# Attention stage of a streaming encoder step: query tiles in the keys' pool, 12 gate blocks ahead, one head's division on ScalarE, LayerNorm sums on GpSimd, the merge kept in PSUM banks

## The chip, the cores and the metric

The kernel runs on one core of one Trainium2 chip. The metric is device time in microseconds of one launch. Three runs of the kernel before took 2397.39, 2404.95 and 2409.07 us; the median is 2404.95 us. Engines are named as the profile names them: PE (TensorE, with PEld for its weight loads), DVE (VectorE), ACT (ScalarE), POOL (GpSimd), and SP, whose queue issues every DMA of this kernel.

## The reference: what is computed

One layer of a streaming encoder on 1024 prompt frames and 64 sample frames (which see 128 cached frames), model width 1024:

```python
h = x + 0.5 * swiglu(rms(x, ffn1_norm), ffn1_w_in, ffn1_w_out)
u = rms(h, mix_norm)
q, k, v, qi, ki, wi, conv_in, gate = split(u @ w_in)
# branch A: per query keep the top 256 keys (48 for the sample) by the indexer's score
attn = softmax(q k^T / 8 over the kept keys) v            # 8 heads of 64, 2 key heads
# branch B
c  = ca * sigmoid(cb)                                     # conv_in = [ca | cb], 512 channels
dc = causal_depthwise_conv31(c) + conv_b
conv_out = silu(layernorm(dc, ln_g, ln_b)) @ conv_w_out
g_a, g_c = split(sigmoid(gate + b_gate))                  # 1024 columns each
h = h + (g_a * (attn @ attn_w_out) + g_c * conv_out) @ w_out
h = h + 0.5 * swiglu(rms(h, ffn2_norm), ffn2_w_in, ffn2_w_out)
y = rms(h, final_norm)
```

It also returns the new keys, values, indexer keys and the last 30 convolution rows.

## The kernel before, in words

Activations lie transposed: channels on the 128 partitions, frames along the free dimension. Every product is done in three passes with operands split in a high and a low part (`mm3`, L135 to L138: high by high, high by low, low by high); ACT makes the high part (L118, L152), DVE or POOL the low part (L119, L153). Outside the attention stage the frames are cut in four blocks of 272; in and around it in three chunks of 364, 362 and 362 (`CHUNKS`).

The program has five stages: the first FFN; the input projection with the indexer scores and the convolution; the search for each query's threshold (DVE, with branches on the data that handle ties, L972 to L1029); the attention stage; and the rest (the last merge and output projection, the second FFN, the final norm). The change lies in the attention stage and just ahead of it.

**Gates.** A gate block (`gates`, L1046) is one 128-column block of the gate weights: per chunk, 8 x 3 = 24 matmuls into a PSUM bank, a tanh by ACT from that bank (L1052, tile `sg`), and a DMA of it to DRAM (L1053). There are 16 blocks of three such steps. `GPRE` = 14 of them run ahead of the attention stage, beside the search on DVE; the other two run inside it.

**Attention.** A unit (`Pair`) is one query tile and two heads; tiles are taken in the order 7, 6, 8, 5, 4, 3, 2, 1, 0, four units each. `soft` (L1079) makes a unit's probabilities: scores by PE into one of three `lg` banks (L1099, L1100), mask added and maximum taken by DVE into tile `pr` (L1102, a custom operation), maximum scaled by DVE (L1110), exponential with its sum by ACT for each of the two heads (L1112), reciprocals by DVE (L1114), and the division: head 0 by POOL, head 1 by DVE (L1116, `SC = 'PV'`). `turn` (L1119) transposes one slot (up to two blocks of 128 keys of both heads) on PE into one of two `pt` banks (L1126) and splits it: high part by ACT (tile `ph`), low part by DVE (tile `pl`). `values` (L1138) multiplies by the values two slots later (L1146, L1147) and sends the result to DRAM. There are 84 slots. The queries of a tile are loaded by `load_q` (L683): four DMAs into `raw`, a cast by ACT (L691) and a subtraction by DVE (L692) into tile `qt`. The first tile's `qt` comes from pool `ak`, which also holds the keys; the next one's from `ap_`, the attention pool, which is opened after the search's pools are closed; then they alternate. Each pool has one.

**Fill.** After each slot `fill` (L1328) advances other work, so that PE has something to do while a unit's softmax is under way. `RATE` says how many steps per slot: 0.75 in `conv_part` (the LayerNorm of chunk 2 beside the last two gate blocks, seven steps; then `conv_out` of the three chunks, eight steps of 12 matmuls each, beside the LayerNorms of the other two), 0.7 in `merge_part` (`merge` of chunk 2, nine steps of which eight have 12 matmuls, and `wout` of chunk 2, eight steps of 24), 2.0 in `last_part` (`merge` of chunk 1). A merge waits until its chunk's query tiles are done (`need_of`, `ready`). The fill's results go through two PSUM banks (`psf`).

**LayerNorm** (`norm`, L1182). The chunk comes from DRAM as four channel tiles (`lx`); DVE adds two pairs (L1189); PE sums over the partitions with a matrix of ones (L166, `colsum`); PE spreads the mean back (L175); DVE adds it (L1198), ACT squares (L1199), DVE adds pairs again (L1200), PE sums, DVE takes the reciprocal root and scales by it and the gain (L1211); then ACT takes tanh (L1213), and two DVE operations with the bias make x + b times (1 + tanh) (L1214, L1216); then the split (L152, L153, tiles `ch`, `cl`).

**Merge** (`merge`, L1244). Per 128 columns: gate `ga` and the stored convolution part `mpt` come from DRAM, PE projects the attention result into a bank `p` (`ps` in the profile), DVE makes (1 + ga) * p into `ga` (L1263) and adds half of `mpt` (L1264), then the split (tiles `xh`, `xl`).

The order of instructions on each engine is fixed when the program is built, by a scheduler that works from its own estimate of durations; each engine runs its list in order and waits on semaphores. A wait that the scheduler did not foresee therefore holds everything that stands behind it on that engine.

## Time and profile before

| | us |
|---|---|
| median of three runs | 2404.95 (2397.39 to 2409.07) |
| the profiled execution, its own time | 2402.76 |
| its span, first to last instruction | 2400.7 |
| PE busy in the span | 2296.5 (96%) |
| DVE busy | 1696.4 (71%) |
| POOL busy | 1412.6 (59%) |
| ACT busy | 1169.0 (49%) |
| mean granted PE clock | 0.984 |

The first score matmul of the attention stage starts at 1233.21 us of the span, and the last value matmul at 1543.21 us. In the rows below, `out<-in` are tiles by the program's names, `x24` a count, and "idle before" the time that the engine stood still just ahead of such instructions, with the one whose end released them. PE's busy time is that of overlapping matmuls; a run of equal matmuls is better priced from start to start. In a table of windows the columns are the busy time of PE, its weight loads, DVE, ACT and POOL, then the granted PE clock (1.00 is full), the share of the DMA engines and GB/s.

### The profile page before, as it was taken

What the parts mean: (1) busy time and instruction counts of PE and PEld (TensorE: products, weight loads), DVE (VectorE), ACT (ScalarE), POOL (GpSimd) and SP (SyncE); (2) the same over time, 40 slices, a digit from 0 to 9 for tenths busy, and PEclk for the clock granted to TensorE, in tenths of its full rate; (3) what the DMA queues carried; (4) which work ended last, traced back from release to release, by engine and by line L of the source; (5) the groups of instructions that cost most, each with busy time, mean ns of one, the idle gap of its engine ahead of it and who ended that gap; (6) DMA issues with size and microseconds to landing.
All of it is one profiled execution on the core that took longest, in us unless ns stands there. A gap on an engine that the chain in (4) does not pass through costs nothing.

```text
span 2400.7 us, 44002 instructions
## 1 busy us (share of the span) xinstructions
PE 2296.5 (96%) x16610; PEld 2266.0 (94%) x16610; DVE 1696.4 (71%) x3776; ACT 1169.0 (49%) x2238; POOL 1412.6 (59%) x873
## 2 busy tenths in 40 slices
PE   7999999999999999999799989799999999999998
PEld 6999999999999999999788888799999999999997
DVE  7766667766668387689727977768666678676666
ACT  6333445444436446887345555545433444434343
POOL 5455555555557786879754455457555555545554
PEclk9999999999999999999999989999999999999999
DMA  5332233223223444233233456653222321332233
GB/s 192 106 108 94 95 100 125 89 89 106 90 92 127 138 127 135 83 120 120 67 99 98 144 164 178 212 172 111 83 94 99 105 101 62 124 107 93 94 97 117
DMA packets 130407, 273.44 MB, mean 114 GB/s; under 512 B 17936, under 2 KB 77200, under 8 KB 130192
## 3 DMA queue, kind: packets, MB, share of 16 engines
q1 hardware_dynamic: 130192, 270.61, 35.0%
q8 instruction: 131, 2.15, 0.4%
q14 instruction: 84, 0.69, 0.1%
HBM read 231.87 MB, written 38.75 MB: 113 GB/s over the span
## 4 chain that ended last, share of the span: by engine, by line
PE 42%; DVE 5%; DMA 2%; issue 1%; ACT 0%; POOL 0%; DVEq 0%; SPq 0%; ACTq 0%
PE ps L136 13%; PE ps L138 13%; PE ps L137 13%; PE pt L1126 1%; DMA ga<-d_g 1%; PE ps L166 1%; DVE pr L1102 1%; PE pv L1146 0%; DVE pl L153 0%; PE pv L1147 0%; DVE ga L1264 0%; PE lg L1099 0%; DMA ar<-d_at 0%; PE lg L1100 0%; DVE t L211 0%
## 5 line engine op out<-in xcount | busy, mean ns | idle before, releaser
L119 POOL TENSOR_TENSOR wlo<-raw,whi 128x1024 fp32r<-128x1024 f32 (+1 forms) x187 | 438.5, 2350 | 360.6 <-ACT whi L118 353.0
L136 PE MATMUL ps<-x,wp 128*128 128x272 f32 x1760 | 506.4, 289 | 3.0 <-ACT wp L152 2.9
L137 PE MATMUL ps<-x,wp 128*128 128x272 f32 x1760 | 505.1, 288 | 0.0
L136 PE MATMUL ps<-x,whi 128*128 128x272 f32 (+2 forms) x1544 | 483.3, 313 | 22.7 <-ACT sg L1052 14.0
L138 PE MATMUL ps<-x,wp 128*128 128x272 f32 x1760 | 503.4, 290 | 1.4 <-DVE wp L153 1.1
L138 PE MATMUL ps<-x,wlo 128*128 128x272 f32 (+2 forms) x1544 | 481.5, 312 | 0.0
L137 PE MATMUL ps<-x,whi 128*128 128x272 f32 (+2 forms) x1334 | 412.9, 310 | 0.9 <-POOL x L153 0.9
L136 PE MATMUL ps<-gh,whi 128*128 128x272 f32 x1408 | 400.0, 289 | 6.8 <-DVE spare L284 5.0
L137 PE MATMUL ps<-gl,whi 128*128 128x272 f32 x1408 | 405.2, 289 | 0.0
L138 PE MATMUL ps<-gh,wlo 128*128 128x272 f32 x1408 | 404.2, 289 | 0.0
L153 POOL TENSOR_TENSOR wlo<-raw,whi 128x1024 fp32r<-128x1024 f32 x88 | 219.5, 2495 | 258.8 <-ACT whi L152 258.8
L136 PEld LDWEIGHTS ps<-x,wp 128*128 128x128 f32 x1760 | 331.2, 188 | 3.9 <-ACT wp L152 3.8
L138 PEld LDWEIGHTS ps<-x,wp 128*128 128x128 f32 x1760 | 328.8, 188 | 2.9 <-DVE wp L153 2.3
L137 PEld LDWEIGHTS ps<-x,wp 128*128 128x128 f32 x1760 | 331.4, 188 | 0.0
L136 PEld LDWEIGHTS ps<-x,whi 128*128 128x128 f32 x1544 | 293.6, 190 | 25.4 <-ACT sg L1052 14.7
L153 POOL TENSOR_TENSOR wp<-s,wp 128x512 fp32r<-128x512 f32 x176 | 257.2, 1462 | 98.3 <-ACT wp L152 98.2
L118 ACT ACTIVATE whi<-raw 128x1024 fp32r<-128x1024 f32 (+1 forms) x187 | 190.6, 1020 | 226.2 <-PE ps L137 103.4
L680 POOL TENSOR_TENSOR ac<-ac,pd 128x559 f32<-128x559 f32 x180 | 264.6, 1470 | 53.5 <-ACT pd L679 27.6
L428 DVE SCALAR_TENSOR_TENSOR h<-ps,h 128x272 f32<-128x272 f32 x384 | 164.3, 437 | 186.3 <-PE ps L138 185.6
L138 PEld LDWEIGHTS ps<-x,wlo 128*128 128x128 f32 x1544 | 293.5, 190 | 1.0
L136 PEld LDWEIGHTS ps<-gh,whi 128*128 128x128 f32 x1408 | 263.6, 189 | 7.9 <-DVE spare L284 5.5
L138 PEld LDWEIGHTS ps<-gh,wlo 128*128 128x128 f32 x1408 | 266.3, 189 | 0.0
(254 smaller groups left out, 4818.9 us busy)
## 6 DMA issues: line engine op xcount, KB each, us to landing
raw<-wf SPq DMA_DIRECT2D x337, 512.0 KB, 3.4
raw<-wf SPq DMA_DIRECT2D x32, 384.0 KB, 3.2
d_g<-sg SPq DMA_DIRECT2D x32, 181.0 KB, 1.9
d_h<-h SPq DMA_DIRECT2D x2, 2176.0 KB, 10.8
y<-t SPq DMA_DIRECT2D x32, 136.0 KB, 1.9
raw<-d_q SPq DMA_DIRECT2D x32, 128.0 KB, 3.1
raw<-d_qi SPq DMA_DIRECT2D x24, 128.0 KB, 3.0
d_g<-sg SPq DMA_DIRECT2D x16, 182.0 KB, 3.6
```

What stands on the lines that cost most here:

```text
L118: nc.scalar.activation(hi[:, :n], raw[:, :n], AF.Copy)
L119: self.weng.tensor_tensor(lo[:, :n], raw[:, :n], hi[:, :n], op=ALU.subtract)
L136: t.matmul(out, wh, xh, start=first, stop=False)
L137: t.matmul(out, wh, xl, start=False, stop=False)
L138: t.matmul(out, wl, xh, start=False, stop=last)
L153: (eng or nc.vector).tensor_tensor(lo, x, hi, op=ALU.subtract)
L166: self.nc.tensor.matmul(ps[:, b * P:(b + 1) * P], x[:, t0:t0 + P], self.ones, start=i == 0, stop=i == len(tiles) - 1)
L428: nc.vector.scalar_tensor_tensor(x, p, 0.5, x, op0=ALU.mult, op1=ALU.add)
L680: nc.gpsimd.tensor_tensor(ac, ac, pd, op=ALU.add)
L1102: nc.vector.tensor_tensor_reduce(p[:, b * pw:(b + 1) * pw], o, bias[:rows, bo:bo + pw], 1.0, -3e38, op0=ALU.add, op1=ALU.max, accum_out=mb ...
L1126: nc.tensor.transpose(pt[:kn, o:o + r], u.pr[hh][:, kk:kk + kn], ident[:r, :r])
```

## The change

Seven edits, all in or around the attention stage:

1. `load_q` of the attention takes its `qt` from `ak`, two buffers there, for all tiles; none is in `ap_`.
2. `GPRE` 14 becomes 12: four gate blocks instead of two run inside the attention stage.
3. The fill has five parts instead of three. `gate_part` runs five gate steps alone, then the LayerNorm of chunk 2 beside the other seven; `conv_part` is the convolution's projection; `merge_part` and `wout_part` are apart; `RATE` is 0.5, 1.0, 1.0, 0.5, 1.0 steps per slot.
4. Head 1's division goes from DVE to ACT (a copy with a scale per row).
5. The two pair sums of each LayerNorm go from DVE to POOL.
6. The LayerNorm's bias: ACT adds it (`Identity` with a bias), and one DVE operation multiplies by (1 + tanh), in place of two DVE operations.
7. In `merge`, the first DVE operation writes its result back into the PSUM bank, and the second reads it there.

```diff
-SC = 'PV'
-GPRE = 14
+GPRE = 12
-RATE = (0.75, 0.7, 2.0)
+RATE = (0.5, 1.0, 1.0, 0.5, 1.0)
...
-                    qts[u.i] = load_q(ak, d_q, u.t0, rows, (ak, ap_)[AORD.index(u.i) % 2], 1)
+                    qts[u.i] = load_q(ak, d_q, u.t0, rows)
...
-                            for e in range(2):
-                                {'P': nc.gpsimd, 'V': nc.vector}[SC[e]].tensor_scalar(u.pr[e], u.pr[e], sm[:rows, e:e + 1], None, op0=ALU.mult)
+                            nc.gpsimd.tensor_scalar(u.pr[0], u.pr[0], sm[:rows, 0:1], None, op0=ALU.mult)
+                            nc.scalar.activation(u.pr[1], u.pr[1], AF.Copy, scale=sm[:rows, 1:2])
...
-                nc.vector.tensor_tensor(s[:, 0:2, :], x[:, 0:2, :], x[:, 2:4, :], op=ALU.add)
+                nc.gpsimd.tensor_tensor(s[:, 0:2, :], x[:, 0:2, :], x[:, 2:4, :], op=ALU.add)
...
-                nc.vector.tensor_tensor(s[:, 0:2, :], s[:, 0:2, :], s[:, 2:4, :], op=ALU.add)
+                nc.gpsimd.tensor_tensor(s[:, 0:2, :], s[:, 0:2, :], s[:, 2:4, :], op=ALU.add)
...
-                    nc.vector.scalar_tensor_tensor(s[:, t, :], x[:, t, :], par("lnb", t), s[:, t, :],
+                    nc.scalar.activation(x[:, t, :], x[:, t, :], AF.Identity, bias=par("lnb", t))
+                    nc.vector.scalar_tensor_tensor(x[:, t, :], s[:, t, :], 1.0, x[:, t, :],
                                                    op0=ALU.add, op1=ALU.mult)
-                    nc.vector.scalar_tensor_tensor(x[:, t, :], x[:, t, :], par("lnb", t), s[:, t, :],
-                                                   op0=ALU.add, op1=ALU.add)
...
-                    nc.vector.scalar_tensor_tensor(ga, ga, 1.0, p, op0=ALU.add, op1=ALU.mult)
-                    nc.vector.scalar_tensor_tensor(ga, mpt, 0.5, ga, op0=ALU.mult, op1=ALU.add)
+                    nc.vector.scalar_tensor_tensor(p, ga, 1.0, p, op0=ALU.add, op1=ALU.mult)
+                    nc.vector.scalar_tensor_tensor(ga, mpt, 0.5, p, op0=ALU.mult, op1=ALU.add)
...
+            def gate_part():
+                steps = gates(gorder[GPRE:], ak, 2)
+                for _ in range(3 * (16 - GPRE) - 7):
+                    next(steps)
+                    yield
+                lp = C["pool"] = self.pool(cx, "ln", 1)
+                yield from both(norm(2, lp, lp), steps)
+                act_es.close()
...
-            parts = [conv_part(), merge_part(), last_part()]
-            need_of = (None, 2, 1)
+            parts = [gate_part(), conv_part(), merge_part(), wout_part(), last_part()]
+            need_of = (None, None, 2, None, 1)
```

How the built programs differ at the places that matter, engine by engine. A row is an instruction with its line, the tiles it writes and reads, and the semaphores on which it waits; `DVE_sequencer` is one that DVE raises when it has left the search's branches. Lines between L35 and the LayerNorm's sums are one lower in the changed kernel.

First, ACT at the end of the search, before. The row with L691 is the cast of the second query tile; L972 is the place of the search's branch on ACT; L679 belongs to the convolution, L118 to the gates' weights.

```order
L118 ACTIVATE whi<-raw 128x1024 [waits DMAHW4_49,PE_49]
L1052 ACTIVATE sg<-ps,hb 128x362 [waits DMAHW2_49,PE_49]
L679 ACTIVATE pd<-ci,par 128x559 [waits Pool_49] x2
L972 UNCONDITIONAL_BRANCH
L1052 ACTIVATE sg<-ps,hb 128x364 [waits DMAHW3_49,PE_49]
L691 ACTIVATE qt<-raw_15467 128x1024 [waits DVE_sequencer_49,DVE_49]
L679 ACTIVATE pd<-ci,par 128x559 [waits Pool_49] x2
L1052 ACTIVATE sg<-ps,hb 128x362 [waits DMAHW5_49,PE_49]
```

And ACT in the changed kernel, where that cast (now L690) stands, among the search's last rounds (L892 to L895).

```order
L892 ACTIVATE bias,cnt<-Y,cand 128x1024 [waits Activation_49]
L678 ACTIVATE pd<-ci,par 128x559 [waits Pool_49]
L894 ACTIVATE flag<-cnt,thx 128x1 [waits Activation_49]
L678 ACTIVATE pd<-ci,par 128x559 [waits Pool_49]
L690 ACTIVATE qt<-raw_15176 128x1024 [waits DMAHW6_49,DMAHW7_49,DMAHW2_49,DMAHW1_49]
L895 ACTIVATE hibx<-flag,cand 128x1 [waits Activation_49]
L117 ACTIVATE whi<-raw 128x1024 [waits DMAHW5_49,PE_49]
L1051 ACTIVATE sg<-ps,hb 128x362 [waits DMAHW4_49,PE_49]
```

The cast has moved from behind the branch to 52 rows ahead of it, and waits only for its DMAs; its subtraction on DVE moves into the search with it. Behind the branch, which stands on ACT's row 1023 now and on 1021 before, there are only convolution and gate rows.

Second, PE a little after the first scores, before: scores, the LayerNorm's sum (L166), scores, gates.

```order
L1099 MATMUL lg<-kh_13693,qt 128x512 [waits DVE_49]
L1100 MATMUL lg<-kl_13694,qt 128x512
L138 MATMUL ps<-x,wlo 128x364
L1099 MATMUL lg<-kh_13693,qt 128x512 [waits DVE_49]
L1100 MATMUL lg<-kl_13694,qt 128x512
L166 MATMUL ps<-ones,ls 128x128 [waits DMAHW3_49,DMAHW4_49,DMAHW2_49,DMAHW5_49,DMAHW1_49,DMAHW6_49,DMAHW0_49,DMAHW7_49,DVE_sequencer_49,DVE_49]
L166 MATMUL ps<-ones,ls 128x128 x7
L1099 MATMUL lg<-kh_13693,qt 128x512 [waits DVE_49]
L1100 MATMUL lg<-kl_13694,qt 128x512
L136 MATMUL ps<-x,whi 128x362 [waits Activation_49]
```

And PE in the changed kernel at its first transposes (L1125).

```order
L137 MATMUL ps<-x,wlo 128x362
L135 MATMUL ps<-x,whi 128x364 [waits Activation_49]
L136 MATMUL ps<-x,whi 128x364
L137 MATMUL ps<-x,wlo 128x364 [waits Pool_49]
L135 MATMUL ps<-x,whi 128x364
L1125 MATMUL pt<-ident,pr 128x128 [waits DVE_sequencer_49,Pool_49]
L1125 MATMUL pt<-ident,pr 128x128 x7
L1098 MATMUL lg<-kh_13702,qt 128x512 [waits DVE_49]
```

The first score matmul stands on PE's row 8401 before and on 8257 now: 144 gate matmuls (six steps of 24) that stood ahead of it stand behind it. In the changed kernel 19 gate matmuls stand between the third and the fourth score tile, 76 between the first score and the first transpose, and the first LayerNorm sum comes 110 rows after that transpose.

Third, POOL ahead of its first division (L1116, now L1114), before.

```order
L119 TENSOR_TENSOR wlo<-raw,whi 128x1024 [waits DMAHW0_49,PE_49,Activation_49]
L680 TENSOR_TENSOR ac<-ac,pd 128x559 [waits Activation_49,Pool_49] x6
L119 TENSOR_TENSOR wlo<-raw,whi 128x1024 [waits DMAHW4_49,PE_49,Activation_49]
L119 TENSOR_TENSOR wlo<-raw,whi 128x1024 [waits DMAHW7_49,PE_49,Activation_49] x2
L1116 ISA
L1116 TENSOR_SCALAR pr<-pr,sm 128x1024 [waits DMAHW3_49,DVE_sequencer_49,DVE_49]
```

And POOL there in the changed kernel; L1188 is the first LayerNorm sum.

```order
L118 TENSOR_TENSOR wlo<-raw,whi 128x1024 [waits DMAHW3_49,PE_49,Activation_49]
L679 TENSOR_TENSOR ac<-ac,pd 128x559 [waits Activation_49,Pool_49] x6
L118 TENSOR_TENSOR wlo<-raw,whi 128x1024 [waits DMAHW0_49,PE_49,Activation_49]
L1188 TENSOR_TENSOR ls<-lx 128x784 [waits DMAHW2_49,DMAHW3_49,DMAHW1_49,DMAHW4_49,DMAHW0_49,DMAHW5_49,DVE_sequencer_49,DMAHW6_49,DVE_49,DMAHW7_49,Activation_49,Pool_49]
L1114 ISA
L1114 TENSOR_SCALAR pr<-pr,sm 128x1024 [waits DVE_49] x2
```

The LayerNorm sum, which waits for its load from DRAM, now stands in POOL's list ahead of the first division; the later five sums stand between divisions (L1114) and the weights' low parts (L118) in the same way.

More of the change, by code (lines that the diff above doesn't have):

```diff
@@ L1041, in run @@
             AORD = TORD
-            qts = {AORD[0]: load_q(ak, d_q, *ATILES[AORD[0]][:2], qb=1)}
+            qts = {AORD[0]: load_q(ak, d_q, *ATILES[AORD[0]][:2])}
             gorder = [(m, self.woff()) for m in (*range(8, 16), *range(8))]
@@ L1297, in both @@
                     yield
-            def conv_part():
-                with ExitStack() as es:
-                    lp_ = self.pool(es, "ln", 1)
-                    yield from both(norm(2, lp_, lp_), gates(gorder[GPRE:], ak, 2))
-                    act_es.close()
-                    lq = self.pool(es, "lnq", 1, side="right")
+            cx = ExitStack()
+            def gate_part():
[6 more added lines that the diff above has]
+                act_es.close()
+            def conv_part():
+                lp_ = C["pool"]
+                with cx:
+                    lq = self.pool(cx, "lnq", 1, side="right")
                     for c, q in ((2, lq), (1, lp_), (0, None)):
@@ L1311, in merge_part, with wout_part @@
                 yield from merge(2, self.mp)
+            def wout_part():
                 yield from wout(2, h_dram(self.mp))
@@ L1335, in fill @@
                     if next(parts[state[0]], "end") == "end":
-                        if state[0] == 2:
+                        if state[0] == 4:
                             return
```

## The prediction

> **What bounds the kernel now.** The page comes first: which engine fills the span?
>
> ```profile
> span 2400.7 us, 44002 instructions
> PE 2296.5 (96%) x16610; PEld 2266.0 (94%) x16610; DVE 1696.4 (71%) x3776; ACT 1169.0 (49%) x2238; POOL 1412.6 (59%) x873
> ```
>
> PE does, and the change takes no matmul away. It can gain only what PE loses, by standing still or by a slow clock, and that is not spread evenly. The table of windows shows it, cut where PE's state changes:
>
> ```profile
> 1160.00:1187.00 27.00, 26.90 (x162) 26.45 (x160) 20.56 (x52) 10.79 (x16) 24.12 (x13) 1.00 0.23 74
> 1187.00:1201.00 14.00, 0.14 (x1) 0.00 (x0) 7.94 (x11) 2.72 (x4) 0.87 (x1) 0.59 0.00 1
> 1201.00:1233.00 32.00, 30.64 (x168) 30.34 (x168) 0.00 (x0) 14.66 (x23) 20.59 (x14) 0.91 0.40 125
> 1233.00:1543.00 310.00, 278.27 (x1750) 260.80 (x1751) 246.79 (x639) 178.00 (x373) 151.11 (x78) 0.96 0.46 141
> 1543.00:1560.00 17.00, 11.65 (x55) 11.47 (x54) 7.62 (x12) 5.87 (x12) 5.95 (x3) 0.80 1.02 339
> ```
>
> Three losses: a hole of 14 us with a slow clock behind it; the attention stage (1233 to 1543), where PE stands still for 310 - 278.27 = 31.7 us and the clock's mean of 0.96 takes another 0.04 x 310 = 12.4 us, 44.1 us together; and the stage's end, 5.4 us idle. In the stage DVE is the next busiest, 246.79 of 310 us, while between 1201 and 1233 it does nothing at all.
>
> The timelines of three engines explain the hole. First PE (start, duration, then what it waited for), where the first two rows are 24 matmuls apart:
>
> ```profile
> 1166.78 0.33 PE L136 MATMUL ps<-x,whi 128*128 128x364 f32 x1
> ...
> 1170.78 0.33 PE L136 MATMUL ps<-x,whi 128*128 128x362 f32 x1
> ...
> 1201.14 0.67 PE L136 MATMUL ps<-x,whi 128*128 128x362 f32 x1 [14.00 <-ACT sg L1052]
> ...
> 1233.21 0.50 PE L1099 MATMUL lg<-kh,qt 128*128 128x512 f32 x1 [1.44 <-ACT sg L1052]
> ...
> 1234.48 0.39 PE L1100 MATMUL lg<-kl,qt 128*128 128x512 f32 x1
> ```
>
> ACT and DVE at the same place:
>
> ```profile
> 1180.27 0.55 ACT L1052 ACTIVATE sg<-ps,hb 128x364 f32<-128x364 f32 x1
> 1198.28 1.06 ACT L691 ACTIVATE qt<-raw 128x1024 fp32r<-128x1024 f32 x1 [17.46 <-DVEq L1018]
> 1199.24 1.40 ACT L679 ACTIVATE pd<-ci,par 128x559 f32<-128x559 f32 x2
> 1200.55 0.54 ACT L1052 ACTIVATE sg<-ps,hb 128x362 f32<-128x362 f32 x1
> ```
>
> ```profile
> 1195.87 0.82 DVE L1029 SCALAR_TENSOR_TENSOR bias<-Y,bias 128x640 bf16<-128x640 f32 x1
> 1199.37 1.22 DVE L692 TENSOR_TENSOR qt<-raw,qt 64x1024 fp32r<-64x1024 f32 x1 [2.67 <-ACT qt L691]
> 1234.11 0.69 DVE L1102 CUSTOM_DVE_ANT_0 pr<-lg,bias 128x512 f32<-128x512 f32 x1 [33.52 <-PE lg L1100]
> ```
>
> ACT stood for 17.46 us at one cast, that of the second query tile, until DVE left the branches of the search (DVEq L1018). Behind it in ACT's list stood the tanh that frees a gate's bank, so PE ran out of banks for 14.00 us. Then PE still had 168 gate matmuls to do before the first score, and DVE, which had been free since about 1198, waited 33.52 us for it. So the attention stage starts some 35 us later than the search allows.
>
> Last, who holds PE inside the stage: the list of waits, 1233 to 1543 (total, times, longest):
>
> ```profile
> PE ps L136 <- DVE ga L1263: 6.1, 4, 2.6
> PE ps L166 <- DVE ls L1189: 5.9, 3, 3.0
> PE ps L136 <- ACT ah L152: 4.7, 3, 3.7
> PE lg L1099 <- DVE mb L1102: 3.8, 6, 1.8
> PE ps L136 <- ACT ch L152: 3.7, 2, 2.5
> PE pt L1126 <- DVE pl L153: 2.7, 5, 0.8
> PE ps L137 <- POOL cl L153: 1.7, 2, 0.9
> PE pv L1146 <- DVE oh L1153: 1.7, 3, 0.7
> ```
>
> Of these 30.3 us DVE ends 6.1 + 5.9 + 3.8 + 2.7 + 1.7 = 20.2 us. No single wait is long; it is DVE's queue arriving late in many places.
>
> **The change part by part.** Prices come from these groups (busy, mean ns of one), the same stretch:
>
> ```profile
> L119 POOL TENSOR_TENSOR wlo<-raw,whi 128x1024 fp32r<-128x1024 f32 x30 | 74.2, 2476 | 41.5 <-ACT whi L118 39.7 <-DMA gc<-d_g 1.8
> L1116 POOL TENSOR_SCALAR pr<-pr,sm 128x1024 f32<-128x1024 f32 (+8 forms) x36 | 65.7, 1826 | 96.1 <-DVE sm L1114 60.6 <-PE lg L1100 14.1 <-DVE mu L1194 4.8
> L1112 ACT ACTIVATE pr<-pr,mx 128x1024 f32<-128x1024 f32 (+8 forms) x72 | 52.6, 733 | 36.3 <-DVE mx L1110 36.2
> L1116 DVE TENSOR_SCALAR pr<-pr,sm 128x1024 f32<-128x1024 f32 (+8 forms) x36 | 25.2, 700 | 0.5
> L1214 DVE SCALAR_TENSOR_TENSOR ls<-lx,par,ls 128x392 f32<-128x392 f32 (+2 forms) x12 | 9.9, 833 | 0.0
> L1264 DVE SCALAR_TENSOR_TENSOR ga<-mpt,ga 128x362 f32<-128x362 f32 x14 | 9.5, 684 | 0.1
> L1263 DVE SCALAR_TENSOR_TENSOR ga<-ga,ps 128x362 f32<-128x362 f32 x15 | 7.8, 522 | 4.8 <-DMA ga<-d_g 4.6
> L1216 DVE SCALAR_TENSOR_TENSOR lx<-lx,par,ls 128x392 f32<-128x392 f32 (+2 forms) x12 | 7.2, 607 | 0.0
> L1199 ACT ACTIVATE ls<-lx 128x392 f32<-128x392 f32 (+2 forms) x12 | 5.5, 505 | 0.9 <-DVE lx L1198 0.9
> L1189 DVE TENSOR_TENSOR ls<-lx 128x784 f32<-128x784 f32 (+2 forms) x3 | 2.8, 928 | 3.5 <-DMA lx<-d_dc 3.5
> L1200 DVE TENSOR_TENSOR ls<-ls 128x784 f32<-128x784 f32 (+2 forms) x3 | 2.8, 928 | 0.0
> ```
>
> **The start of the stage: query tiles and gate blocks.** Now: from 1187.0 to the first score at 1233.21 are 46.2 us. A gate step of 24 matmuls takes 1170.78 - 1166.78 = 4.00 us, so the 168 are worth 28.0; PE loses 18.2 us here. In the changed order the cast stands ahead of the branch and waits for DMAs alone, so the hole goes. 144 of the 168 matmuls now stand behind the first score, so PE reaches it at 1187.0 + 4.0 = 1191.0. It does three score tiles (six matmuls, five start to start in 1.27 us: 1.5 us) and 19 gate matmuls (3.2 us), and at 1195.7 needs the first `lg` bank back, which DVE frees with its first maximum. DVE comes out of the search at about 1198.3, plus the subtraction of 1.22 us that now lies inside the search, plus 0.69: 1200.2. So the new wait is 1200.2 - 1195.7 = 4.5 us: what is late next is the search itself. For the clock behind it I take 1.5 us: between zero and the 0.09 x 32 = 2.9 us that the 14 us hole cost. (By the Trainium skill, TensorE: Matmul & The Clock Gate, section "What's actually happening", an idle window of about 3.4 us halves the clock for at least as long, which would make 1.7 us, an estimate.) The loss is then 6.0 us in place of 18.2: **12.2 us gained**. Behind that point PE has 57 gate matmuls and nine score tiles, 9.5 + 4.5 us, before its first transpose: until about 1214.2, while the first unit's softmax runs. That covers POOL's late first division; without the cover its wait behind the LayerNorm sum (below) would cost some 3.5 us.
>
> **The fill.** It holds 24 us more PE work (144 matmuls), taken from ahead of the stage, so PE's work as a whole is unchanged. Steps of 24 matmuls are given at 0.5 per slot and steps of 12 at 1.0: 2.0 us of fill in each of the 84 slots. Before, it was 1.5 us beside the convolution (0.75 x 2.0), none while the first merge waited for its tiles, 1.4 in the merge, 2.8 in `wout`, 4.0 at the end. Parts run 26 + 25 + 10 + 18 slots and end near slot 79, so PE's leftover after the last slot is about four merge steps, the cover it has at the end now.
>
> **DVE.** It loses 36 divisions (25.2 us), 24 bias operations for 12 of the kind of L1216 (9.9 + 7.2 - 7.2 = 9.9) and six sums (5.6): 40.7 us of 246.8. The merge's two operations stay; with the bank in place of SBUF the second costs between 522 ns (L1263, which reads a bank) and 684 (now): I take no change, as the bank is held longer by that one operation. There are two banks, so the other one covers it; if it doesn't, PE pays 24 x 0.5 = 12 us.
>
> **ACT.** It gains 36 divisions at 700 (the DVE row) to 733 ns (the exponential of the same tiles), 26.4 us, and 12 bias additions at 505 ns, 6.1 us: 178 becomes 210 us, in a stage of some 300. It is not the bound by busy time. But each division waits for DVE's reciprocal, and what stands behind it on ACT are `ph` copies, weight copies and gates' evictions.
>
> **POOL.** Six sums of 724 to 784 columns: between 0.93 us (DVE's) and 2.48 (L119, 1024 columns); 1.8 by columns. 10.8 us beside 151.
>
> **What PE then loses in the stage.** Nothing in the trace shows this directly. The end that excludes most is zero loss; the other is 44.1 us again. I take half, 22 us: DVE's five waits (20.2 us) fall to about 8, the rest stays near its 10 plus 4 at the LayerNorm; and with fill in every slot fewer stops are long enough to slow the clock, 12.4 becoming 6 at most; some small stalls then remain. **22 us gained.** The end's 5.4 us stays.
>
> Sum: 12.2 + 22 = 34.2 us. The profiled execution took 2402.76 us, 2.06 us more than its span and 2.2 below the median of the runs, 2404.95. 2402.76 - 34.2 = 2368.6: **2369 us**.
>
> **The rivals.**
>
> **The attention chain sets the pace, not PE.** Each slot goes through PE, ACT, DVE and back with two slots of slack. If latency and not DVE's load makes the 44.1 us, it stays, and only the start gains: 2402.8 - 12.2 = 2390.6. For it: no wait in the list exceeds 3.7 us and they have several owners. Against: two thirds of them are DVE's. Chance 0.11.
>
> **The LayerNorm sums hold PE.** POOL's sum stands in a list with divisions (1826 ns) and low parts (2476 ns). If each of six sums comes later by its own extra 0.9 us and one such row, 1.8 to 2.5, PE waits 6 x 3.0 = 18 us at L166: 2369 + 18 = 2387. The Trainium skill (GPSIMD Engine Reference, section "Engine selection") advises against such adds on GpSimd, as about twice slower than VectorE. The rows say the same of this size (1.8 against 0.93 us); what decides is if PE waits there. PE's list has the first such sum 110 rows after the first transpose, which speaks against. Chance 0.09.
>
> **ACT becomes the brake: slower.** In the same list of waits, ACT's longest entry is the one for DVE's maximum:
>
> ```profile
> ACT pr L1112 <- DVE mx L1110: 36.2, 24, 3.5
> ```
>
> That is 1.5 us each. If the 36 divisions each hold ACT for 1.5 us more and PE's banks and transposes stand behind them, that is 54 us on PE: 2369 + 54 = 2423. It turns into a loss from 34.2 / 36 = 0.95 us per division on. Against: DVE is lighter, and PE takes a result only two slots later. Chance 0.05.
>
> **PE nearly gap-free.** With 2 us of fill always there, the stage loses a tenth, 4.4 us, and the start keeps its 6: 2402.8 - 12.2 - 39.7 = 2350.9. Chance 0.14.
>
> **How the numbers follow.** The forecast (half the loss, anything from a fifth to three quarters) has 0.58: 2356 to 2380. The four rivals have 0.39, and 0.03 is for what I don't see. The range from 2346 to 2394 holds the forecast, the gap-free case and both middling rivals, and leaves out the slow one. A measurement of this kernel can tell some 0.5%, 12 us, from no change: faster means below 2393. The first rival lies within 2.4 us of that, so half of it counts as the same, with a fourth of the second: faster 0.84, same 0.10, slower 0.06.
>
> **What would show it.** Right: no wait of ACT at the cast of a query tile; a first score near 1191, DVE's first maximum near 1199.5, PE's wait there of 3 to 6 us; first transpose near 1215; the last value matmul some 34 us earlier, near 1509; in the stage PE idle near 15 us and its clock near 0.98; DVE's busy time 40 us down. Wrong: the first maximum still after 1215 (the start); PE's waits on L1188 or L1199 above 10 us (the sums); ACT's waits for reciprocals with PE's waits on `ph` or `sg` behind them (the brake); or PE idle of 30 us again with no new owner (the chain).

## The result and the profile after

The changed kernel took 2390.23 us, median of 7 runs (2388.05 to 2391.79). Its ratio to the kernel before is 0.9948, interval 0.9932 to 0.9964, so it is 12.5 us faster (0.0052 x 2404.95), where 36 were forecast. The ratio is over the six runs of the kernel before that lie between 2397.39 and 2409.07 us; a seventh, at 10873.34 us, is left out of it. The profiled execution took 2389.32 us, and these are its span and engines:

```profile
span 2387.5 us, 43966 instructions
PE 2291.5 (96%) x16610; PEld 2262.8 (95%) x16610; DVE 1658.5 (69%) x3722; ACT 1197.3 (50%) x2286; POOL 1418.2 (59%) x879
```

PE does the same matmuls. The same windows as before show what came true and what did not:

```profile
1160.00:1187.00 27.00, 24.73 (x149) 24.43 (x148) 21.53 (x58) 13.28 (x20) 26.29 (x14) 1.00 0.18 62
1187.00:1201.00 14.00, 8.63 (x53) 8.33 (x51) 9.79 (x8) 6.87 (x10) 13.61 (x7) 0.93 0.19 65
1201.00:1233.00 32.00, 22.00 (x111) 20.52 (x112) 15.99 (x39) 16.32 (x23) 20.86 (x12) 0.77 0.29 97
1233.00:1543.00 310.00, 280.06 (x1788) 265.29 (x1787) 201.83 (x560) 201.48 (x418) 149.07 (x83) 0.95 0.49 146
1543.00:1560.00 17.00, 17.00 (x93) 17.00 (x93) 2.74 (x6) 4.80 (x9) 5.34 (x3) 0.88 1.00 347
```

In the stage DVE fell from 246.79 to 201.83 us, 45 us, somewhat more than the 40.7 worked out. Yet PE still stands idle for 310 - 280.06 = 29.9 us there (31.7 before), at a clock of 0.95 (0.96). From 1543 to 1560 PE has no gap any more (before, it was busy for 11.65 of these 17 us).

At the start the hole is still there; it only has a new place. PE's timeline (the row above the gap is its last gate matmul), then ACT's and POOL's beside it:

```profile
1195.31 0.32 PE L137 MATMUL ps<-x,wlo 128*128 128x362 f32 x1
1211.00 0.79 PE L1098 MATMUL lg<-kh,qt 128*128 128x512 f32 x1 [15.37 <-ACT sg L1051]
```

```profile
1205.65 0.54 ACT L1051 ACTIVATE sg<-ps,hb 128x362 f32<-128x362 f32 x1
1206.89 0.76 ACT L678 ACTIVATE pd<-ci,par 128x559 f32<-128x559 f32 x1 [0.70 <-POOL ac L679]
1208.79 0.76 ACT L678 ACTIVATE pd<-ci,par 128x559 f32<-128x559 f32 x1 [1.14 <-POOL ac L679]
1209.46 1.04 ACT L117 ACTIVATE whi<-raw 128x1024 fp32r<-128x1024 f32 x1
1210.41 0.54 ACT L1051 ACTIVATE sg<-ps,hb 128x362 f32<-128x362 f32 x1
```

```profile
1201.02 10.63 POOL L679 TENSOR_TENSOR ac<-ac,pd 128x559 f32<-128x559 f32 x6
1211.61 2.37 POOL L118 TENSOR_TENSOR wlo<-raw,whi 128x1024 fp32r<-128x1024 f32 x1
```

ACT no longer waits at a query's cast. But the score's banks are those of the last gates ahead of it. Their tanh (L1051) stand on ACT between the products for the last convolution's taps (L678), and each product waits for POOL's sum (L679) to give a buffer back. So the last tanh comes at 1210.41, when POOL's taps are nearly through, and PE waits 15.37 us for it. The hole before had hidden this: while ACT stood, POOL stood too. Its row in the kernel before:

```profile
1200.13 6.06 POOL L680 TENSOR_TENSOR ac<-ac,pd 128x559 f32<-128x559 f32 x4 [15.38 <-ACT pd L679]
```

Who holds PE inside, 1233 to 1543:

```profile
PE pv L1145 <- DVE oh L1152: 6.6, 4, 4.2
PE lg L1098 <- DVE mb L1101: 4.3, 5, 2.0
PE ps L135 <- ACT ch L151: 4.2, 2, 2.4
PE pt L1125 <- DVE pl L152: 3.4, 3, 2.3
PE ps L165 <- POOL ls L1188: 3.0, 1, 3.0
PE ps L135 <- DVE ga L1262: 2.5, 3, 1.2
PE ps L135 <- ACT ah L151: 2.4, 1, 2.4
PE ps L135 <- DVE hr L1274: 1.5, 2, 1.0
PE ps L135 <- DVE oh L1152: 0.9, 1, 0.9
```

It is a list of the same kind as before with other owners. DVE still ends 6.6 + 4.3 + 3.4 + 2.5 + 1.5 + 0.9 = 19.2 us of it, where it ended 20.2. And DVE, though lighter, waits more for the fill's operands: for gate loads 10.4 us where it waited 4.6, and for the loads of h's rows (hr), for which it did not wait before, another 10.4. Of its own waits in the stage (longer in total are only those for ACT's exponentials, 16.9, for PE's transposes, 13.9, and for ACT's high parts of these, 12.7):

```profile
DVE hr L1274 <- DMA hr<-d_h: 10.4, 2, 6.6
DVE ps L1261 <- DMA ga<-d_g: 10.4, 9, 2.5
DVE hr L1274 <- PE ps L137: 9.0, 4, 4.5
```

### The profile page after: what moved, and what is told of

The parts are those of the page before. It is cut to its first block, busy times and chain, and to the rows that moved or that the text cites. A ratio compares the mean times of both kernels' runs of the same rounds, so it can differ in the third digit from the quotient of the medians.

```text
span 2387.5 us, 43966 instructions
## 1 busy us (share of the span) xinstructions
PE 2291.5 (96%) x16610; PEld 2262.8 (95%) x16610; DVE 1658.5 (69%) x3722; ACT 1197.3 (50%) x2286; POOL 1418.2 (59%) x879
## 5 line engine op out<-in xcount | busy, mean ns | idle before, releaser
L118 POOL TENSOR_TENSOR wlo<-raw,whi 128x1024 fp32r<-128x1024 f32 (+1 forms) x187 | 433.8, 2325 | 356.1 <-ACT whi L117 345.3
L135 PEld LDWEIGHTS ps<-x,whi 128*128 128x128 f32 x1544 | 293.0, 190 | 12.2 <-DVE sg L622 3.5
L679 POOL TENSOR_TENSOR ac<-ac,pd 128x559 f32<-128x559 f32 x180 | 270.5, 1503 | 39.2 <-ACT pd L678 13.7
## 6 DMA issues: line engine op xcount, KB each, us to landing
d_h<-h SPq DMA_DIRECT2D x2, 2176.0 KB, 10.7
```

The lines of the kernel that those rows point to most:

```text
L118: self.weng.tensor_tensor(lo[:, :n], raw[:, :n], hi[:, :n], op=ALU.subtract)
L135: t.matmul(out, wh, xh, start=first, stop=False)
L679: nc.gpsimd.tensor_tensor(ac, ac, pd, op=ALU.add)
```

## The experiments

**The measure.** For each matmul, the trace gives the distance to the start of the next; what it exceeds the usual distance of its form at full clock is counted as PE's loss. It is summed from 1180 to the first transpose (start), to the last value matmul (inside), and over the 100 us behind that (end). Ratios are to the kernel before in the same batch, whose median was 2399 to 2405 us. The losses are of one execution, and runs of one kernel differ by 4 to 12 us, so the ratios give the verdict and the losses the place.

| kernel | ratio (interval) | start | inside | end |
|---|---|---|---|---|
| before | 1 | 23.6 | 52.9 | 16.1 |
| after | 0.9948 (0.9932–0.9964) | 20.5 | 52.0 | 5.4 |
| q_only | 0.9950 (0.9933–0.9967) | 7.3 | 53.2 | 15.4 |
| no_q | 0.9986 (0.9974–0.9999) | 27.2 | 54.6 | 5.3 |
| gpre13 | 0.9925 (0.9905–0.9945) | 8.0 | 52.8 | 5.3 |
| gpre14 | 0.9943 (0.9925–0.9961) | 7.9 | 56.4 | 5.8 |
| short_conv | 0.9904 (0.9876–0.9931) | 9.9 | 52.4 | 5.4 |
| div_dve | 0.9967 (0.9948–0.9985) | 19.2 | 50.7 | 12.0 |
| sum_dve | 0.9963 (0.9947–0.9980) | 17.3 | 52.3 | 5.6 |
| merge_sbuf | 1.0000 (0.9985–1.0016) | 18.3 | 59.9 | 12.3 |
| old_fill | 0.9922 (0.9896–0.9948) | 18.9 | 42.8 | 9.8 |
| old13 | 0.9941 (0.9920–0.9962) | 14.6 | 47.0 | 5.4 |
| old13_div | 0.9950 (0.9934–0.9967) | 14.7 | 50.3 | 8.5 |
| old13_pref | 0.9896 (0.9866–0.9925) | 14.2 | 41.7 | 5.6 |
| bank_only | 0.9998 (0.9980–1.0016) | 21.4 | 56.1 | 12.0 |
| mx_act | 0.9946 (0.9926–0.9966) | 21.1 | 47.1 | 9.5 |
| wlo_dve | 0.9947 (0.9931–0.9962) | 18.6 | 50.2 | 5.2 |
| phase | 1.0001 (0.9985–1.0017) | 18.0 | 43.1 | 23.6 |
| phase_pref | 0.9933 (0.9907–0.9959) | 20.4 | 45.4 | 4.8 |
| best | 0.9885 (0.9860–0.9910) | 14.0 | 37.2 | 3.5 |

### The start of the stage

The first theory was that the last convolution holds the start; its rival, that the chain of score, softmax and transposes does.

q_only is the kernel before with the first edit alone, 14 gates ahead:

```
-            qts = {AORD[0]: load_q(ak, d_q, *ATILES[AORD[0]][:2], qb=1)}
+            qts = {AORD[0]: load_q(ak, d_q, *ATILES[AORD[0]][:2])}
...
-                    qts[u.i] = load_q(ak, d_q, u.t0, rows, (ak, ap_)[AORD.index(u.i) % 2], 1)
+                    qts[u.i] = load_q(ak, d_q, u.t0, rows)
```

> The kernel before with edit 1 alone (all query tiles in the keys' pool; 14 gate blocks ahead, all else as before). Theory T, the convolution holds the start: in the changed kernel the wait of ACT at the query cast is gone, but PE waits 15.5 us at the first score for a bank whose tanh stands on ACT behind the last convolution taps, which POOL paces until about 1211 us. With 14 gates ahead PE reaches the first score only near 1215 to 1219, after those taps, so edit 1 alone gives nearly the whole gain: hole below 4 us, 2385 to 2393 us. Theory C, the attention chain sets the pace and the start is worth what the chain gains: the first score comes 14 to 18 us earlier than before and the time follows it, 2387 to 2391, the stage's inner loss unchanged near 44 us. Both agree on the sum; the hole and the stage's loss tell them apart, and the time tells what the other six edits add.

no_q is the changed kernel with the same edit undone:

> The changed kernel with edit 1 undone (query tiles alternate between the two pools). Theory T: ACT stands at the cast until DVE leaves the search (about 1200 us), POOL's taps stand with it and end near 1217 to 1219, and with only 12 gates ahead PE waits for the last tanh from 1195 to about 1218: 2395 to 2401 us, 5 to 10 over the changed kernel. Theory C: as the chain starts 7 us later, 2397. The prediction's reading (the cast costs 14 us and its clock): 2404 to 2408.

gpre13 and gpre14 are the changed kernel with one number changed:

```
-GPRE = 12
+GPRE = 13
```

> The changed kernel with 13 gate blocks ahead. Theory T: PE reaches the first score 12 us later than in the changed kernel, near 1207, so the wait there falls from 15.5 us to about 4 and its slow clock goes too: 2374 to 2381 us. Theory C: the chain starts when the search and the convolution let it, near 1211 either way, and the fill loses 12 us of work: 2388 to 2392, no change.

> The changed kernel with 14 gate blocks ahead. Theory T: no wait at the first score (reached near 1219 instead of 1211), the 20 us of hole and slow clock gone, but the stage has 24 us less fill, so its inner loss grows by up to half of that: 2374 to 2385 us. Theory C: the chain starts 8 us later than in the changed kernel: 2396 to 2400.

The first edit takes 16 us off the start's loss (23.6 to 7.3), and undoing it costs 7 (20.5 to 27.2). With one more gate ahead PE has work until the taps end, and in place of one wait of 15.4 us gpre13 has these between 1180 and 1237, 5.5 us:

```profile
PE ps L135 <- ACT sg L1051: 3.9, 3, 1.8
PE lg L1098 <- ACT sg L1051: 1.6, 1, 1.6
```

The times of no_q, gpre13 and gpre14 (2396.68, 2380.23 and 2384.79 us) lie in the first theory's ranges; for the last two the rival had 2388 or more.

short_conv leaves 16 of the 30 taps of the last half of the last convolution out:

```
-                    for j in range(1, CW):
+                    for j in range(1, CW - 16 if t == 2 and s0 else CW):
```

> The changed kernel, but the last half of the last convolution on GpSimd leaves out 16 of its 30 taps, so that GpSimd and ScalarE finish it some 30 us earlier. Convolution theory (the last gates' tanh stand on ScalarE behind the taps, their banks are the first score's, and GpSimd's taps slow VectorE's search where they run beside it): PE's wait of 15.4 us at the first score falls below 5, the search's ties take 19 us in place of 23.7, and the time falls by about 10, to 2380. Attention chain theory (the search or the softmax sets the start): the first maximum stays at 1212 and the time within 3 us of 2390. Inside the stage both expect the loss of 52 us again.

The tanh's wait all but goes, and what is late next is the search on DVE, as the prediction had it (5.3 us where it said 4.5, with the first maximum at 1202.37 where it said 1200.2):

```profile
PE lg L1098 <- DVE mb L1101: 5.3, 1, 5.3
PE lg L1098 <- ACT sg L1051: 1.5, 1, 1.5
```

The ratio fell by 0.0044, 10.6 us, as the convolution theory said, and the inside kept its 52 us. The rival falls for the start. The second half of the claim holds too: the search's ties took 18.1 us (1181.93 to 1200.06) in place of 23.9 (1183.64 to 1207.54). Two of its operations on DVE in the changed kernel, the second of which is its last, and the first of them in short_conv:

```profile
1195.24 2.30 DVE L1028 SCALAR_TENSOR_TENSOR bias<-Y,bias 128x1024 bf16<-128x1024 f32 x1
1205.67 1.87 DVE L1028 SCALAR_TENSOR_TENSOR bias<-Y,bias 128x640 bf16<-128x640 f32 x1
```

```profile
1191.71 1.22 DVE L1028 SCALAR_TENSOR_TENSOR bias<-Y,bias 128x1024 bf16<-128x1024 f32 x1
```

### One edit undone at a time

The load theory is the prediction's: PE's loss inside follows DVE's busy time. The order theory is that DVE works its list in order and stands at operands that are not there yet, whatever its load.

div_dve puts the second head's division back on DVE, sum_dve the LayerNorm's sums:

```
-                            nc.scalar.activation(u.pr[1], u.pr[1], AF.Copy, scale=sm[:rows, 1:2])
+                            nc.vector.tensor_scalar(u.pr[1], u.pr[1], sm[:rows, 1:2], None, op0=ALU.mult)
```

> The changed kernel, with the second head's 36 divisions on DVE again instead of ACT. Load theory (PE's loss inside the attention stage follows DVE's busy time, as the prediction had it: 22 us for 40.7 us): 36 x 0.70 = 25.2 us more of DVE cost 25.2 x 22 / 40.7 = 13.6 us, so 2390.2 + 13.6 = about 2404. Order theory (DVE works its list in order and stands at operands of the fill that aren't there yet, so that its busy time hardly counts): 2388 to 2393, and DVE's waits in the stage become shorter by about what its work becomes longer.

```
-                nc.gpsimd.tensor_tensor(s[:, 0:2, :], x[:, 0:2, :], x[:, 2:4, :], op=ALU.add)
+                nc.vector.tensor_tensor(s[:, 0:2, :], x[:, 0:2, :], x[:, 2:4, :], op=ALU.add)
...
-                nc.gpsimd.tensor_tensor(s[:, 0:2, :], s[:, 0:2, :], s[:, 2:4, :], op=ALU.add)
+                nc.vector.tensor_tensor(s[:, 0:2, :], s[:, 0:2, :], s[:, 2:4, :], op=ALU.add)
```

> The changed kernel, with the six sums of the LayerNorm on DVE again instead of GpSimd. Load theory: six sums of 0.93 us are 5.6 us of DVE, 5.6 x 22 / 40.7 = 3 us more: 2393. Order theory: no change, 2388 to 2392, and PE's wait at the first sum (3.0 us in the changed kernel) stays or changes its name.

The ratios lie 0.0019 (div_dve) and 0.0015 (sum_dve) above the changed kernel's, with intervals that overlap. For the division the load theory's figure was 0.0057; for the sums it was 3 us, 0.0013, so sum_dve does not tell the two theories apart. The loss inside did not grow (50.7 and 52.3), though in div_dve DVE had 218.13 us of work from 1233 to 1543 instead of 201.83. What div_dve has more of is the end's loss, 12.0 us where the changed kernel has 5.4.

old_fill cuts the fill into its three old parts again and gives it the old rates:

```
-RATE = (0.5, 1.0, 1.0, 0.5, 1.0)
+RATE = (0.75, 0.7, 2.0)
...
-            parts = [gate_part(), conv_part(), merge_part(), wout_part(), last_part()]
-            need_of = (None, None, 2, None, 1)
+            parts = [conv_part(), merge_part(), last_part()]
+            need_of = (None, 2, 1)
```

> The changed kernel, with the fill cut into its three old parts at their old rates (0.75, 0.7, 2.0), and 12 gates ahead as changed. The question is which edit took the 10 us at the end of the stage, where PE lost 15.9 us in 100 before and 5.4 after. If it is the new fill: the end loses 15 again, about 2400. If it is the merge in banks: the end stays at 5 and the time at 2390. Order theory for the inside of the stage: it moves by several us, since other loads arrive at other places, with DVE's work the same; load theory: inside, no change.

Its ratio is lower than the changed kernel's, 0.9922, though the intervals overlap. With DVE's work nearly as in the changed kernel (205.83 us in the window) the loss inside is 9 us less, more than the division moved it. The end has 9.8 us: neither the 15 of one answer to the run's question nor the 5 of the other.

merge_sbuf writes the merge's first product to SBUF again:

```
-                    nc.vector.scalar_tensor_tensor(p, ga, 1.0, p, op0=ALU.add, op1=ALU.mult)
-                    nc.vector.scalar_tensor_tensor(ga, mpt, 0.5, p, op0=ALU.mult, op1=ALU.add)
+                    nc.vector.scalar_tensor_tensor(ga, ga, 1.0, p, op0=ALU.add, op1=ALU.mult)
+                    nc.vector.scalar_tensor_tensor(ga, mpt, 0.5, ga, op0=ALU.mult, op1=ALU.add)
```

> The changed kernel, with the merge's first product written to SBUF again and not to its bank. The prediction put this edit at no change. So 2388 to 2392, and PE's wait for the merge within 2 us. Rival: it took part of what PE lost at the end of the stage (15.9 us to 5.4, of which the old fill gives back 4.4): then the end loses 10 or more again, and the time is 2395 or above. The second operation should take about 0.68 us again instead of 0.52.

That is 0.0052 slower, the whole gain of the change, and spoke for the rival. The merge's second operation shows why it might be the edit itself (duration in ns, least, median, longest; merge_sbuf, then the changed kernel):

```profile
L1262 DVE SCALAR_TENSOR_TENSOR ga<-mpt,ga x24: 507/531/2770, 1442.9 to 1610.6; 128x362 f32<-128x362 f32 x16, 128x364 f32<-128x364 f32 x8
```

```profile
L1262 DVE SCALAR_TENSOR_TENSOR ga<-mpt,ps x24: 503/532/534, 1445.3 to 1601.7; 128x362 f32<-128x362 f32 x16, 128x364 f32<-128x364 f32 x8
```

With both inputs in SBUF eight of the 24 take 0.8 to 2.77 us; with one in a bank none does. So there was a third theory, the port: DVE held behind GpSimd.

### The old fill with more

old13 is old_fill with 13 gates ahead; old13_div puts the division back in it; old13_pref issues the loads of the merge and the output projection one step ahead, with three buffers instead of two:

```
+                def load(m):
+                    ga = mp_.tile([P, WMAX], F32, name="ga", tag="ga", bufs=3)[:, :w]
...
+                nxt = load(0)
                 for m in range(8):
...
+                    ga, mpt = nxt
+                    nxt = load(m + 1) if m < 7 else None
```

> The changed kernel with the fill's old parts and rates, and 13 gates ahead instead of 12. If the hole at the first score (13 gates: start's loss 8 us instead of 19 to 21) and the new fill's cost inside the stage (43 us of loss with the old fill instead of 52) are two separate things, they add up: span 2379.8 - 11 = 2369, time about 2371. If one more gate ahead only moves the loss into the stage, as 14 gates did with the new fill: about 2381, as with 12 gates and the old fill.

> As the run with the old fill and 13 gates, with the second head's 36 divisions on DVE again. With the new fill the 25 us of DVE changed the loss inside the stage by nothing (52.0 to 50.7). Load theory in a weaker form (the lighter DVE pays once the fill no longer stands in its way: 52.9 to 42.8 us of loss for 40.7 us of DVE): 25.2 x 10.1 / 40.7 = 6 us slower than that run. Order theory: within 3 us of it, since the loss comes from where the fill's steps fall and not from DVE's load.

> As the run with the old fill and 13 gates, but the merge's and the output projection's loads (gate, convolution part, row of h) are issued one step ahead, with three buffers instead of two. Order theory in its narrow form (DVE stands at loads of the fill that come late, and scores and transposes stand behind it): DVE's waits for these loads (6.4 us in the run with the old fill, 24 in the changed kernel) go, PE's wait for the merge's first operation (10.1 us) falls by about half, 5 us faster than that run. Rival (DVE has room there, the loads are not what PE waits for): within 2 us of it.

The two gains do not add up: old13 is no faster than old_fill. About half of what the start gained is taken by the LayerNorm's first sum on POOL, which is then early enough for PE to wait for it, 1212 to 1237:

```profile
PE ps L165 <- POOL ls L1188: 5.2, 1, 5.2
```

The division again costs nothing that can be told (0.9950 against 0.9941). The loads ahead gave 0.0045, 10.8 us, twice what was expected; PE's wait for the merge's operations fell from 9.8 to 3.0 us (1237 to 1660: old13, then old13_pref):

```profile
PE ps L135 <- DVE ga L1262: 9.8, 7, 2.9
```

```profile
PE ps L135 <- DVE ga L1268: 3.0, 2, 2.5
```

### The port, the load, or the order

bank_only is the kernel before with the merge in banks alone. mx_act moves the scaling of the maxima to ACT:

```
-                            nc.vector.tensor_scalar(mx[:rows, :], mm, -0.125, None, op0=ALU.mult)
+                            nc.scalar.activation(mx[:rows, :], mm, AF.Copy, scale=-0.125)
```

wlo_dve computes the weights' low parts on DVE during the stage; phase starts the fill half a step earlier:

```
+            self.weng = nc.vector
             attention(units, fill)
+            self.weng = nc.gpsimd
```

```
-            state = [0, 0.0]
+            state = [0, 0.5]
```

> The kernel before, with one edit of the change alone: the merge's first product goes to its bank. Port theory (a DVE operation with both inputs in SBUF stands until GpSimd's running operation with two inputs ends; with one input in a bank it does not): the second operation of the merge goes from 0.77 to 0.53 us on average and its longest from 2.77 to below 0.6, PE's wait for the merge (11.5 us from 1235 to 1660) falls by more than half, and the time by 6 to 10 us, to about 0.997 of before. The prediction's step (no change, or a loss of up to 12 us since the bank is held longer): 1.000 or above.

> The changed kernel, with the scaling of the maxima (two numbers per row, 36 times) on ACT instead of DVE. Port theory: these operations take 0.16 us when GpSimd is idle and up to 1.4 beside its low parts, 8 us in all, and every softmax stands behind them; without them PE's loss inside the stage falls by 2 to 5 us: 2385 to 2388. Load theory: 5.8 us of DVE work less, 3 us faster. Rival (the maxima are not what anyone waits for): 2390.

> The changed kernel, with the weights' low parts computed on DVE instead of GpSimd while the attention stage runs (30 to 50 operations of 128x1024). Load theory, the prediction's: at least 30 x 1.2 = 36 us more of DVE, 36 x 22 / 40.7 = 19 us slower: 2409 or above. Port theory: GpSimd's operations that hold DVE go (20 us of held DVE time), and DVE has 100 us to spare: within 8 us of 2390. If DVE's operations between two holds shrink to their own length and PE's loss stays at 52, the holds are not what PE pays for either.

> The changed kernel, with the fill starting half a step earlier and nothing else: a control for what a new order of the same instructions alone does, since the order is made anew for each kernel. If order alone moves little: 2388 to 2392, and differences of 4 us between single edits can be ascribed to them. If it moves the time by 5 us or more, only the larger ones can.

wlo_dve takes 62 of GpSimd's 149 us of work out of the stage and gives DVE a group of 34.7 us. Its window and the added group:

```profile
1233.00:1543.00 310.00, 281.08 (x1793) 267.70 (x1792) 220.45 (x583) 198.19 (x412) 86.70 (x57) 0.94 0.49 149
```

```profile
L118 DVE TENSOR_TENSOR wlo<-raw,whi 128x1024 fp32r<-128x1024 f32 x26 | 34.7, 1333 | 4.7 <-ACT whi L117 4.7
```

Its time is the changed kernel's (0.9947), and the loss inside 50.2, with DVE at 220.45 us instead of 201.83. The load theory's figure was 2409. Nothing was gained by the port either, with POOL at 86.70 us instead of 149.07. That the two only cancelled is unlikely, since in div_dve load alone raised no loss inside. But the port was relieved in part only: of the operations that are held most, the scalings of the maxima, 20 took 6.9 us here and 9.6 in the changed kernel. mx_act takes all of these off DVE and stayed in the interval of the changed kernel (0.9946). In bank_only the merge's second operation is never held (506 to 534 ns), and still PE's wait for the merge did not fall (13.6 us from 1235 to 1660, 11.5 before) and the ratio is 0.9998. So the port's price for PE is not seen in any of the three, and merge_sbuf's 12 us were not the merge's own.

phase shows what a new order alone can cost. A control in which the same work comes half a step earlier has the ratio 1.0001: it lost the whole gain, as merge_sbuf did. (In merge_sbuf's trace no wait like the one below is found, so where its order lost the time is not known.) Its profiled execution, 2395.33 us, is the fastest of its ten, and still shows where. SP's list at the stage's end, then DVE's and PE's rows:

```profile
1526.71 1.38 SPq L1361 DMA_DIRECT2D h<-d_h  x2
1528.18 3.71 SPq L1258 DMA_DIRECT2D mpt<-d_mp  x1
1531.95 0.61 SPq L1361 DMA_DIRECT2D h<-d_h  x1
1532.61 3.99 SPq L1249 DMA_DIRECT2D ar<-d_at  x1
1536.70 0.38 SPq L1256 DMA_DIRECT2D ga<-d_g  x1
```

```profile
1545.46 0.54 DVE L1261 SCALAR_TENSOR_TENSOR ps<-ga,ps 128x362 f32<-128x362 f32 x1 [8.50 <-DMA ga<-d_g]
```

```profile
1549.07 0.64 PE L135 MATMUL ps<-xh,whi 128*128 128x362 f32 x1 [15.90 <-DVE ga L1262]
```

The three loads of h (L1361, 1448 to 1456 KB each) went into SP's list ahead of the merge's small ones. The gate's load came out at 1536.70, DVE stood 8.50 us for it, and PE 15.90 us behind DVE. In the changed kernel the loads of h are issued at 1541.99, behind all but one of that merge's gate loads, and PE has no such wait.

phase_pref is phase with the loads one step ahead, as in old13_pref:

> As the run with the fill half a step earlier (2400, PE idle for 15.9 us at the stage's end for the merge, whose gate load was issued behind 4.3 MB of h in SP's list), with the merge's and the output projection's loads issued one step ahead. Queue theory (late loads of the fill are what an unlucky order costs): the 15.9 us go, the end loses 5 to 8 us instead of 23.6, DVE's waits for the merge's gate loads fall by more than half, and the time comes to 2380 to 2385. If the stall has another cause, it stays: 2395 to 2400.

The 15.9 us are gone (end's loss 23.6 to 4.8), and the ratio falls from 1.0001 to 0.9933, a median of 2382.18 us. This is the queue theory's figure. DVE's waits for the merge's gate loads fell from 13.4 to 1.8 us (1235 to 1560), and in SP's list the loads of h, from 1534.60 on, stand behind all but one of these gate loads again. The order is new here too; that the loads issued ahead mended it is read from the entries' places, with no second control.

best is old13_pref with the sums on DVE and mx_act's edit:

> The run with the old fill, 13 gates and loads one step ahead (0.9896 of before), with two more edits: the LayerNorm's sums on DVE again (PE waited 5.2 us for the first one on GpSimd at the start of the stage) and the scaling of the maxima on ACT. If both waits are PE's: 5 us from the first, up to 3 from the second, about 0.9865 of before, 2366 to 2369. If the new order eats it: 0.987 to 0.992. Slower than that would say that the gain of the loads issued ahead was the order's.

2370.78 us, 0.9885 (0.9860 to 0.9910), the fastest of all, though its lead on old13_pref (0.0011, 2.6 us) is within the intervals. PE's wait for the first sum stayed at 4.8 us and only changed its owner, since the sum stands at its load, not at GpSimd (DVE's waits, 1205 to 1240):

```profile
DVE ls L1188 <- DMA lx<-d_dc: 5.3, 1, 5.3
```

## Why the prediction was wrong

**The hole at the cast goes: right.** The cast stands at 1103.62 now, with 0.43 us of wait, and by q_only this edit alone takes 16 us off the start's loss when PE has 14 gates ahead.

**The new wait of 4.5 us, and so 12.2 us gained at the start: wrong.** The step that failed is "so PE reaches it at 1187.0 + 4.0 = 1191.0. It does three score tiles": it takes the first three banks of the scores as free and puts no wait ahead of the first score. PE came to the first score at 1195.63, since 51 gate matmuls and not 24 were left at 1187.0, and stood there until 1211.00. (That 1195.7 is in the prediction too is chance; there it is the arrival at the fourth score tile.) The first banks were not free: they waited for the gates' tanh, which stand on ACT behind products that wait for POOL's taps. The wait was 15.4 us, the first maximum came at 1212.38 and the first transpose at 1231.6 (1200.2 and about 1214 forecast). The prediction followed ACT's list to the cast and took what stood behind it as freed; POOL had stood for 15 us in the trace of before, so its taps still had to come.

The other half of that step was off as well. The search was to let DVE go at 1198.3 + 1.22 = 1199.5; its last operation ended at 1207.54. The taps, which now run beside its ties, are 5.8 us of this (23.9 against 18.1 in short_conv); the ties also began 6.0 us later than before (1183.64, 1177.64 before), for which no run was made. So an estimate for free banks, from these rows, is still a wait of some 8 us: the fourth tile at 1195.63 + 1.5 + 3.2 = 1200.3, the first maximum not ended before 1207.54 + 0.69 = 1208.2. The clock behind the hole was put at 1.5 us; by the prediction's own working it is (1 - 0.77) x 32 = 7.4, though 10 us of that window lie in the hole. By the loss, the start gained 3.1 us. short_conv shows that the prediction had named the next wait rightly: without the taps PE waits 5.3 us for DVE.

**Half of the 44.1 us inside: wrong.** The step is "DVE's five waits (20.2 us) fall to about 8", taken from the owners of PE's waits. They are 19.2 us now. DVE did become 45 us lighter and the loss stayed (52.9 to 52.0); 16 us more on DVE (div_dve) or 19 (wlo_dve) did not raise it either. The clock's part, "12.4 becoming 6 at most", is 0.05 x 310 = 15.5 us. An owner in the list of waits is the engine that came last, which does not say that it had too much to do: DVE's own list has it standing at loads, at PE and at ACT. That this is why the loss stayed is shown for single waits, as in phase, and argued for the rest.

**The end's 5.4 us stay: wrong the other way.** The loss behind the last value matmul fell from 16.1 to 5.4, most of the measured gain: 10.7 us, beside 3.1 at the start and 0.9 inside. No single edit accounts for it. The place of the loads of h in SP's list is shown as the cause in phase alone. It is not what the kernel before lost there: its loads of h came at 1543.72, behind six of the merge's eight gate loads, and PE's wait of 5.4 us was for DVE, which stood at no load but took 2.33 us, beside GpSimd, for a split that takes 0.53 elsewhere (phase, 1548.84):

```profile
1544.72 2.33 DVE L153 TENSOR_TENSOR al<-ar,ah 128x364 fp32r<-128x364 f32 x1 [0.67 <-ACT ah L152]
```

Why the end is shorter in the changed kernel stays open.

**The rivals.** The first one's 2390.6 is the time that was measured, and half of its reason held: the stage's loss did stay whatever DVE's load. But most of the 12 us came from the end and not from the start, so that its number came out is luck. The LayerNorm's sum cost 3.0 us and not 18. ACT gained 23.5 us of work, and PE's waits for it in the stage are 6.8 us where they were 8.4. The merge in banks is a "no change" by bank_only, and a 12 us loss to undo by merge_sbuf: both are within what order alone does. No gap-free PE was seen in the changed kernel.

**What stays open.** Which of the orders is good was not settled. The order is made anew for every kernel; across these kernels the inside lies between 37 and 60 us, and phase alone moved it by 9 us and the end by 18. So differences of single edits below 10 us or so are not ascribed to them here, old_fill's and old13_pref's among them, and a small price of DVE's load is not excluded; phase_pref's 16 us (0.0068) are more than that. The 37 us that are left in the best kernel have many owners.

## What to carry to other kernels

When a wait goes, read the list of the engine behind it to the next entry that waits for somebody, and ask what that somebody did during the old wait: here POOL stood too, and its work came back as the new hole. An engine named in many short waits is not thereby too busy; before its load is cut, look at what its own list stands for. In a kernel whose order is made by a scheduler, time a control that changes nothing but the order before crediting an edit with less than that, and issue small loads of the fill ahead of large ones on the same queue.

## What the runs showed of the hardware

DVE's operations on SBUF do not only slow down beside GpSimd's, some wait for their end. In the kernel before, a scaling of two numbers per row, 0.16 us at other times, took 2.27:

```profile
1495.73 2.27 DVE L1110 TENSOR_SCALAR mx<-mb 128x2 f32<-128x2 f32 x1
```

```profile
1495.58 2.40 POOL L119 TENSOR_TENSOR wlo<-raw,whi 128x1024 fp32r<-128x1024 f32 x1 [2.52 <-ACT whi L118]
```

It ended at 1498.00 and POOL's at 1497.98. The Trainium skill (SBUF — State Buffer, section "Who interferes with whom") says that a tensor_scalar on DVE can take a mode in which it and an instruction on GpSimd exclude each other, and that the later one then blocks until the first ends; the trace agrees to 0.02 us. By the same section of the Trainium skill a DVE instruction with two SBUF inputs contends with a GpSimd instruction that reads SBUF. The traces agree in part. In the kernel before, the four of the merge's second operation that started beside POOL's division (L1116, one input) took 517 to 523 ns, as without it, and five beside its low parts (two inputs) 803 to 2771. But one input is no safeguard: in the changed kernel a DVE operation that takes 549 to 555 ns three times took 1.27 us beside a division.

```profile
1302.95 1.27 DVE L1214 SCALAR_TENSOR_TENSOR lx<-ls,lx 128x392 f32<-128x392 f32 x1 [0.35 <-ACT lx L1213]
```

```profile
1302.80 2.52 POOL L1114 TENSOR_SCALAR pr<-pr,sm 128x896 f32<-128x896 f32 x1 [15.06 <-DVE sm L1113]
```

Which of GpSimd's operations hold which of DVE's is not settled here. Along the search they cost 5.8 us (23.9 against 18.1 in short_conv). In the stage no run's time shows a price: wlo_dve took part of the holds away and mx_act the scalings, both at the changed kernel's time. One hold, the 2.33 us above, does stand right ahead of a wait of PE.
